# A layer's modulation in front of the recurrence's projections, and two block inverses with tiles of their own

## The chip, the cores and the metric

The kernel is one program on one core of a Trainium2 chip. What counts is the device time of one execution in microseconds (us). A core has engines that each run their own list of instructions in order: TensorE (PE, matrix products into the accumulator memory PSUM), VectorE (DVE), ScalarE (ACT), GpSimd (POOL) and SyncE (SP, which here only issues transfers from main memory, DMAs, into the on-chip memory SBUF). They meet at semaphores: an instruction waits until the data that it reads is there and the buffer that it writes is free.

## The reference

Two models run one after the other on a sequence `x` of 512 positions and 1024 channels. The change lies in the second, a two-layer model whose last layer is an RWKV-7 mixer. Cut to what matters:

```
mod = silu(c) @ mod_w[1] + mod_b[1]              # 6*1024 numbers: shift, scale, gate of the mixer, then of the FFN
u   = rmsnorm(x) * (1 + scale) + shift
xx  = 0.5 * (u shifted left + u shifted right) - u
k, v, r = (u + xx*mix[j]) @ w_rkv[j]             # 512x1024 by 1024x1024 each
decay_d = f(tanh(xw @ w1[d]) @ w2[d]); a_d = g((xa @ a1[d]) @ a2[d]); g = sigmoid(xg @ g1) @ g2
S_t = S_{t-1} * decay_t + (S_{t-1} @ -kk_t) (kk_t * a_t) + v_t k_t     # per head, forward and reversed
y_t = S_t @ r_t
x = x + gate * (readout(y) @ wo);   x = x + gate2 * swiglu(modulated x)
```

The gate of the mixer and the numbers of the FFN are only read after the recurrence.

## The kernel before

The recurrence is computed in blocks of 64 positions. Within a block the steps depend on each other through a triangular matrix for each head, which is inverted beforehand; the scan over the blocks is then matrix products. `rwkv_x` does this for `x`, after the same has been done for the context (the *context scan*, whose last instructions are L2583 on PE and L2587 on DVE). Its stages:

- `rwkv_branches` (L2071 and on): the norm of `x`, the mixes `u + xx*mix` (L2075, DVE), and linears of 1024 by 1024 in 8 column tiles, each weight tile loaded (`wraw<-rwkv_wrkv`, 512 KB) and split into a high and a low part (`whi` on ACT, `wlo` on DVE), then three products for every pair of tiles (L178 to L180). First comes the linear of k, with three narrow products beside it that the text calls loras: `lora_w`, `lora_a`, `lora_g`, each 24 matmuls into PSUM tag `aux`. The copy L2167 ends `lora_g`, the last of them. The linear of r and the rest follow.
- `rwkv_pairs` for direction 0, then `rwkv_values`; then `rwkv_inverse` for direction 0 (*inverse 0*), `rwkv_pairs` for direction 1 (which completes the matrix `AT1` with L2358), and `rwkv_inverse` for direction 1 (*inverse 1*). `self.pinv` (3 PSUM banks) is another pool for inverse 1 than for inverse 0.
- `rwkv_scan`, whose first products with the inverse are L2556 and L2558. Its products that need no inverse (L2526, L2540 on PE, L2531 and L2534 on DVE) may run earlier.

An inverse begins with transposes (L2382) and copies into `Am` (L2388 on ACT, L2390 on DVE), then a *chain* of 31 steps on DVE in which each step reads the one before (L2398 a product into `stmp`, L2400 a subtraction from `Tm`), and then a *tail*: transposes and small products on PE (L2410, L2430, L2447) whose results DVE and ACT copy out in turns (L2418, L2438, L2454 on DVE). A pool with one buffer for a tag makes a new tile of that tag wait for the last read of the one before: within an inverse, `TR` takes the tag of `Am`, and `US` that of `Tm`.

`modulation(1, nm1, 12, ...)` computes the last eight blocks (512 columns each) of the second layer's modulation, in two groups of four. For each of 32 loads:

```
raw = wraw()                                  # a buffer of tag wmod
nc.sync.dma_start(raw, w[:, g * 4:g * 4 + 4, c0:c0 + 256])           # L1418, 512 KB on SP's queue
for k in range(4):
    nc.tensor.matmul(ps[r:r + 32, ...], sc[:, c:c + 32], raw[:, k, :], ..., tile_position=(0, r))   # L1421
```

After 16 loads ACT copies the sum (`fmod`, L1427), PE multiplies it with a selection matrix (L1434), and DVE adds the bias (L1439). In the trace a load's four matmuls are eight records of L1421. The last group also gives `aff` (L1449, L1450). Nothing in `rwkv_x` reads the result before the readout.

The order of instructions on each engine is set by a scheduler that simulates the program; code that is written earlier is preferred where several instructions are ready. What came out is read from the compiled order below. `self.psums(sb, 3, 2)` gives three PSUM banks of tag `mm` and two of `aux` for the time of `rwkv_branches`.

Of the kernel before, what the change touches and what calls it, by code (L numbers as in the profile page):

```python
# [20 lines left out]
P = 128  # L21
# [82 lines left out]
class Kern:  # L104
# [2646 lines left out]
    def rwkv_x(self, x, rs, xs, xp, xd, sx):  # L2751
        nc = self.nc
        R = {}
        tile = lambda st, name, shape, side=None: self.t(self.pool(st, name, side=side), shape, tag=name)
        with ExitStack() as st:
            self.rp = self.pool(st, "rpx")
            self.rq = self.pool(st, "rqx")
            sv, sb = ExitStack(), ExitStack()
            self.weights_pool(sv, 2, 1024)
            self.work_pool(sv, 6)  # L2760
            self.nbc = 1
            ha = self.pool(sv, "heapv")
            v = self.fork(S)
            v.psums(sv, 2, 1, side="right")
            self.psums(sb, 3, 2)
            sh = ExitStack()
            self.rwkv_branches(x, S, 0, R, rs, (self.pool(sh, "heapb", side="right"), ha), xp)
            sh.close()
            sb.close()

            sr, sp_ = ExitStack(), ExitStack()
            A = [P, 32, 2, 64]
            AT = [tile(sr, "AT0", A, "right"), None]
            self.psums(sp_, 3, 2)
            sp = self.pool(sp_, "pairx", side="right")
            self.work_pool(sp_, 3, side="right")
            self.rwkv_pairs(R, S, 0, 0, AT[0], 0, sp)
            v.rwkv_values(R, S, 0)
            sv.close()
            si, s1 = ExitStack(), ExitStack()  # L2780
            self.pinv, self.pinv_tag = self.pool(si, self.nm("pinv"), 3, PSUM, "right"), "inv"
            DT = [tile(st, "DT0", [P, 64, 64]), None]
            AT[1] = tile(s1, "AT1", A)
            ip = self.pool(s1, "inv")
            self.rwkv_inverse(AT[0], DT[0], ip)
            self.rwkv_pairs(R, S, 0, 1, AT[1], 0, sp)
            sp_.close()
            sr.close()
            xs.close()
            DT[1] = tile(sr, "DT1", [P, 64, 64], "right")  # L2790
            sp = self.pool(sr, "scanx", side="right")
            sc = ExitStack()
            self.pmm = self.pool(sc, self.nm("scm"), 2, PSUM)
            si.close()
            self.paux = self.pool(sc, self.nm("sca"), 3, PSUM, "right")
            self.pinv = self.pool(s1, self.nm("pinv"), 3, PSUM)
            swm = ExitStack()
            wm = self.pool(swm, "wmod3", 1, side="right")
            self.rwkv_inverse(AT[1], DT[1], ip, 1)
            self.modulation(1, self.nm1, 12, (lambda: self.t(self.pmm, [P, 512], tag="aux"),  # L2800
                                              lambda: self.t(wm, [P, 4, 256], tag="wmod", bufs=4),
                                              lambda: self.t(wm, [P, 512], tag="fmod")))
            swm.close()
            s1.close()

            Y = [self.t(self.rq, [P, KC, 2, 2, 64], tag=f"rk{h}") for h in range(2)]
            self.weights_pool(st, 2)
            n = S // 64
            lag = self.lag
            steps = []  # L2810
            for i in range(n + lag):
                steps += [(0, i)] * (i < n) + [(1, i - lag)] * (i >= lag)
            with ExitStack() as s2:
                side = self.fork(S)
                side.work_pool(s2, 7)
                self.pyr = self.pool(s2, self.nm("scy"), 1, PSUM)
                side.paux = self.pmm
                self.rwkv_scan(R, S, 0, [(DT[0], 0), (DT[1], 0)], Y, sp, steps, side, self.pool(s2, "bon"))
            sr.close()
            sc.close()  # L2820
            self.psums(st, 4, 4)
            self.work_pool(st, 8)
            side = self.fork(S)
            side.work_pool(st, 6)
            self.heap(st, 18)
            xp = self.pool(sx, "xfin", side="right")
            x = []
            for k in range(KC):
                x.append(self.t(xp, [P, S], tag=f"x{k}"))
                nc.sync.dma_start(x[k], xd[k])  # L2830
            self.rsx = self.rwkv_readout(R, Y, x, side)
            return x
# [42 lines left out]
```

## Time and profile before

| | us |
|---|---|
| median of 3 runs (lowest, highest) | 3390.59 (3382.8, 3393.72) |
| profiled execution: its own time | 3386.3 |
| profiled execution: span | 3384.5 |
| PE busy | 3031.5 |
| DVE busy | 1901.3 |
| ACT busy | 1295.7 |
| mean granted TensorE clock, of full speed | 0.932 |

The span runs from the first to the last instruction of the profiled execution; its own time is 1.8 us longer. Busy times are sums over the whole span: an engine that is busy nine tenths of the time on average can still stand idle for tens of microseconds in one stage, so the stages around the change are read one by one. A row of windows (groups 1 and 10 below) gives for a stretch its limits and length, then the busy time (and the number of instructions) of PE, of its weight loads, of DVE, ACT and POOL, then TensorE's granted clock as a share of full speed, the busy share of the DMA engines, and GB/s.

### The profile page before, as it was taken

Reading aid. Unit: us, or ns where it says so; the run is one execution under the profiler, and the core shown is the slowest. Engines: PE = TensorE matmul, PEld = TensorE weight load, DVE = VectorE, ACT = ScalarE, POOL = GpSimd, SP = SyncE. Lnnn points to the kernel's source line nnn. Section 1 sums busy time; section 2 is a strip of 40 time slices with the busy share of each in tenths; the row PEclk is TensorE's granted clock in tenths of the full one; section 3 lists DMA queues with packets and bytes.
Section 4 is the critical chain, followed back from the end, with each engine's and each line's share of the span. In section 5 each row is a group of like instructions: output and inputs, shape, how many; then the busy total and the mean of one; then the engine's idle time right before and its main releaser. Section 6 shows DMA issues by size and latency. Waiting matters only on the chain.

```text
span 3384.5 us, 53425 instructions
## 1 busy us (share of the span) xinstructions
PE 3031.5 (90%) x21351; PEld 2320.5 (69%) x21351; DVE 1901.3 (56%) x3118; ACT 1295.7 (38%) x2378; POOL 568.9 (17%) x639
## 2 busy tenths in 40 slices
PE   8989799779999698999799999979977698889999
PEld 5667577544445677787588788866745587778887
DVE  5447553333333767666476776467795644753334
ACT  5335333213232445454344723335672132332222
POOL 2223210311111341000202300020361000310001
PEclk9989899889999799999899999989996589899999
DMA  6553564369997523334544532532775466442322
GB/s 215 172 184 113 191 210 158 112 230 359 360 304 244 170 79 107 110 102 121 171 130 126 146 92 75 136 91 81 207 200 174 112 167 156 129 131 90 97 92 71
DMA packets 537962, 526.04 MB, mean 155 GB/s; under 512 B 72289, under 2 KB 468795, under 8 KB 534640
## 3 DMA queue, kind: packets, MB, share of 16 engines
q1 hardware_dynamic: 512448, 449.77, 43.6%
q0 software_dynamic: 13840, 57.88, 5.1%
q10 hardware_dynamic: 11424, 14.96, 1.8%
q8 instruction: 169, 2.77, 0.4%
q14 instruction: 81, 0.66, 0.1%
HBM read 453.32 MB, written 69.21 MB: 154 GB/s over the span
## 4 chain that ended last, share of the span: by engine, by line
PE 43%; DVE 6%; DMA 5%; issue 3%; ACT 2%; POOL 1%; SPq 0%; ACTq 0%; DVEq 0%; POOLq 0%
PE mm L178 10%; PE mm L179 10%; PE mm L180 10%; PE inv L2447 1%; PE mm L1872 1%; DMA wmod<-mod_w 1%; PE aux L2526 1%; PE mm L2526 1%; DMA v<-vd 1%; PE big L1849 1%; PE aux L2572 1%; PE aux L2583 1%; PE yy L2558 1%; PE aux L1977 1%; DVE wlo L170 1%
## 5 line engine op out<-in xcount | busy, mean ns | idle before, releaser
L178 PE MATMUL mm<-s,whi 128*128 128x512 f32 (+1 forms) x2472 | 871.4, 357 | 48.1 <-ACT whi L169 15.8
L180 PE MATMUL mm<-s,wlo 128*128 128x512 f32 (+1 forms) x2472 | 872.1, 355 | 11.5 <-DVE wlo L170 11.1
L179 PE MATMUL mm<-s,whi 128*128 128x512 f32 (+1 forms) x2472 | 870.9, 353 | 11.4 <-DVE s L170 8.4
L169 ACT ACTIVATE whi<-wraw 128x1024 fp32r<-128x1024 f32 (+2 forms) x444 | 388.2, 882 | 862.1 <-PE mm L179 648.6
L170 DVE TENSOR_TENSOR wlo<-wraw,whi 128x1024 fp32r<-128x1024 f32 (+2 forms) x444 | 456.9, 1036 | 314.8 <-ACT whi L169 309.5
L178 PEld LDWEIGHTS mm<-s,whi 128*128 128x128 f32 x2472 | 473.8, 193 | 145.0 <-ACT whi L169 24.7
L180 PEld LDWEIGHTS mm<-s,wlo 128*128 128x128 f32 x2472 | 475.0, 192 | 90.1 <-DVE wlo L170 18.0
L179 PEld LDWEIGHTS mm<-s,whi 128*128 128x128 f32 x2472 | 475.8, 193 | 84.9 <-DVE s L170 13.2
L270 POOL TENSOR_TENSOR sq<-sq,w 128x512 f32<-128x512 f32 (+1 forms) x64 | 81.5, 1274 | 878.4 <-DVE w L266 787.7
L169 ACT ACTIVATE s<-w 128x512 fp32r<-128x512 f32 (+1 forms) x215 | 114.5, 546 | 90.2 <-POOL w L664 35.0
L170 DVE TENSOR_TENSOR s<-w,s 128x512 fp32r<-128x512 f32 (+1 forms) x215 | 128.4, 614 | 33.5 <-ACT s L169 32.9
L1659 DVE SCALAR_TENSOR_TENSOR x<-mm,mod,x 128x512 f32<-128x512 f32 (+1 forms) x128 | 89.8, 714 | 98.5 <-PE mm L180 97.9
L1330 PE MATMUL aux<-wgu,whi 128*64 128x512 f32 x496 | 131.9, 601 | 0.1
L1855 POOL TENSOR_SCALAR sst<-sst,hrs 128x1 f32<-128x1 f32 x96 | 33.7, 351 | 394.2 <-DVE sst L1853 345.6
L1346 PE MATMUL mm<-wraw,mt 128*64 128x512 f32 x248 | 89.7, 653 | 2.6 <-DVE mt L1340 2.6
L1700 DVE SCALAR_TENSOR_TENSOR w<-w,mm 128x512 f32<-128x512 f32 (+1 forms) x66 | 39.3, 596 | 91.0 <-PE mm L180 90.9
L1330 PEld LDWEIGHTS aux<-wgu,whi 128*64 128x64 f32 x496 | 39.7, 137 | 57.4 <-issue 52.4
L1977 PE MATMUL aux<-ident,pr 128*128 128x128 f32 x384 | 64.6, 277 | 6.5 <-ACT PT L1983 5.6
L1853 DVE TENSOR_REDUCE sst<-big 128x1 f32<-128x768 f32 x64 | 61.0, 953 | 12.9 <-PE big L1849 12.7
L2526 PE MATMUL aux<-LB,sbk 64*128 64x128 f32 x512 | 63.5, 307 | 3.5 <-DVE qq L2534 1.8
L1857 ACT ACTIVATE pr<-big,sst,hrs 128x768 f32<-128x768 f32 x64 | 63.1, 986 | 0.3 <-POOL sst L1855 0.3
L1849 PE MATMUL big<-kk,qs 128*128 128x512 f32 (+1 forms) x256 | 59.5, 356 | 3.9 <-ACT pr L1857 3.8
(711 smaller groups left out, 5365.7 us busy)
## 6 DMA issues: line engine op xcount, KB each, us to landing
wmod<-mod_w SPq DMA_DIRECT2D x80, 512.0 KB, 5.7
wraw<-w_down SPq DMA_DIRECT2D x31, 1024.0 KB, 10.7
wgu<-w_gate SPq DMA_DIRECT2D x56, 512.0 KB, 8.6
wgu<-w_up SPq DMA_DIRECT2D x56, 512.0 KB, 7.7
wraw<-ffn_wg SPq DMA_DIRECT2D x44, 512.0 KB, 3.9
wraw<-ffn_wu SPq DMA_DIRECT2D x44, 512.0 KB, 3.9
wraw<-ffn_wd SPq DMA_DIRECT2D x44, 512.0 KB, 3.8
wraw<-rwkv_wrkv SPq DMA_DIRECT2D x40, 512.0 KB, 4.0
```

The costliest lines, as they stand in the source:

```text
L169: nc.scalar.activation(hi, src, AF.Copy)
L170: nc.vector.tensor_tensor(lo, src, hi.bitcast(F32), op=ALU.subtract)
L178: nc.tensor.matmul(out, lh, rh, start=start, stop=False)
L179: nc.tensor.matmul(out, lh, rl, start=False, stop=False)
L180: nc.tensor.matmul(out, ll, rh, start=False, stop=stop)
L270: nc.gpsimd.tensor_tensor(acc, acc, q, op=ALU.add)
L1330: nc.tensor.matmul(pgu[i * 64:(i + 1) * 64, :], xs[:, k, i * 64:(i + 1) * 64], t[k // 4][:, k % 4, :], start=k == 0, stop=k == KC - 1)
L1346: nc.tensor.matmul(py[i * 64:(i + 1) * 64, :], mt[:, f, i * 64:(i + 1) * 64], d[:, f, q * 512:(q + 1) * 512], start=f == 0, stop=f == 1)
L1659: nc.vector.scalar_tensor_tensor(x[i], ps, self.mod[l][:, q * KC + i, c:c + 1], x[i], op0=ALU.mult, op1=ALU.add)
L1849: nc.tensor.matmul(ps[:, a:a + n], qs[i][:, e, c * P:(c + 1) * P], kk[g][q], start=q == 0, stop=q == 1)
L1977: nc.tensor.transpose(pp[:, k * P:(k + 1) * P], pr[:, (k0 + k) * P:(k0 + k + 1) * P], self.ident)
L2526: nc.tensor.matmul(pv[e][:, p, :NR].rearrange("p q t -> p (q t)"), bk[rows[e], 4 * h + p].rearrange("p s t -> p (s t)"), lb[e][rows[e], 4 ...
```

## The change

The eight blocks of modulation move from behind inverse 1 to the front of `rwkv_branches`. There they take their PSUM from tag `mm`, which the linears use, and have two buffers for their weights where they had four. The two inverses take `Am`, `Tm` and `stmp` from pools of their own (`inv0`, `inv1`), where one pool `inv` served both in turn.

```diff
--- before.py
+++ after.py
@@ -2763,9 +2763,14 @@
             v = self.fork(S)
             v.psums(sv, 2, 1, side="right")
             self.psums(sb, 3, 2)
-            sh = ExitStack()
+            sh, swm = ExitStack(), ExitStack()
+            wm = self.pool(swm, "wmod3")
+            self.modulation(1, self.nm1, 12, (lambda: self.t(self.pmm, [P, 512], tag="mm"),
+                                              lambda: self.t(wm, [P, 4, 256], tag="wmod", bufs=2),
+                                              lambda: self.t(wm, [P, 512], tag="fmod")))
             self.rwkv_branches(x, S, 0, R, rs, (self.pool(sh, "heapb", side="right"), ha), xp)
             sh.close()
+            swm.close()
             sb.close()
 
             sr, sp_ = ExitStack(), ExitStack()
@@ -2781,8 +2786,7 @@
             self.pinv, self.pinv_tag = self.pool(si, self.nm("pinv"), 3, PSUM, "right"), "inv"
             DT = [tile(st, "DT0", [P, 64, 64]), None]
             AT[1] = tile(s1, "AT1", A)
-            ip = self.pool(s1, "inv")
-            self.rwkv_inverse(AT[0], DT[0], ip)
+            self.rwkv_inverse(AT[0], DT[0], self.pool(s1, "inv0"))
             self.rwkv_pairs(R, S, 0, 1, AT[1], 0, sp)
             sp_.close()
             sr.close()
@@ -2794,13 +2798,7 @@
             si.close()
             self.paux = self.pool(sc, self.nm("sca"), 3, PSUM, "right")
             self.pinv = self.pool(s1, self.nm("pinv"), 3, PSUM)
-            swm = ExitStack()
-            wm = self.pool(swm, "wmod3", 1, side="right")
-            self.rwkv_inverse(AT[1], DT[1], ip, 1)
-            self.modulation(1, self.nm1, 12, (lambda: self.t(self.pmm, [P, 512], tag="aux"),
-                                              lambda: self.t(wm, [P, 4, 256], tag="wmod", bufs=4),
-                                              lambda: self.t(wm, [P, 512], tag="fmod")))
-            swm.close()
+            self.rwkv_inverse(AT[1], DT[1], self.pool(s1, "inv1"), 1)
             s1.close()
 
             Y = [self.t(self.rq, [P, KC, 2, 2, 64], tag=f"rk{h}") for h in range(2)]
```

How this stands in the compiled order, first on PE, at the end of the context scan. `aux_..<-v,tk` is the context scan's last product, `L241` the broadcast of the norm's factors, `mm<-s,whi` the linear of k. Before:

```order
L2583 MATMUL aux_17754<-v_3857_17674,tk_17700 64x64
L241 MATMUL aux_20331<-ident_63,rs_20280 128x128 x4
L178 MATMUL mm_20458<-s_20356,whi_20454 128x512
L178 MATMUL mm_20507<-s_20356,whi_20503 128x512
```

and of the changed kernel:

```order
L2583 MATMUL aux_17754<-v_3857_17674,tk_17700 64x64
L1421 MATMUL mm_20331<-wmod_20332,sc_1477 32x256 x4
L1421 MATMUL mm_20331<-wmod_20338,sc_1477 32x256 x4
L241 MATMUL aux_20549<-ident_63,rs_20280 128x128 x4
L1421 MATMUL mm_20331<-wmod_20344,sc_1477 32x256 x4
```

Two loads' matmuls of the modulation (`mm<-wmod,sc`) stand ahead of the broadcast, and more follow it. Further on, the last of the matmuls of `lora_a` (`aux<-s,lw`), the last nine loads of the modulation and the first matmuls of the linear of k, on PE in the changed kernel:

```order
L179 MATMUL aux_20892<-s_20991,lw_4466_20856 128x512
L180 MATMUL aux_20892<-s_20990,lw_4467_20857 128x512
L1421 MATMUL mm_20437<-wmod_20480,sc_1477 32x256 x4
L1421 MATMUL mm_20437<-wmod_20486,sc_1477 32x256 x4
L1421 MATMUL mm_20437<-wmod_20492,sc_1477 32x256 x4
L1421 MATMUL mm_20437<-wmod_20498,sc_1477 32x256 x4
...
L1421 MATMUL mm_20437<-wmod_20522,sc_1477 32x256 x4
L1421 MATMUL mm_20437<-wmod_20528,sc_1477 32x256 x4
L1434 MATMUL mm_20536<-qsel_70,fmod_20534 128x8 x4
L178 MATMUL mm_20676<-s_20574,whi_20672 128x512
L179 MATMUL mm_20676<-s_20575,whi_20672 128x512
```

All 32 loads' matmuls and the second L1434 now stand ahead of the linear's first one; `lora_w` and `lora_a` stand between load 12 and load 24, where they stood among the linear's matmuls. On SP, in the changed kernel, the loads with the fourth weight tile of the linear (`wraw<-rwkv_wrkv`) among them:

```order
L1418 DMA wmod_20462<-mod_w 128x4x256
L186 DMA wraw_20860<-rwkv_wrkv 128x8x128
L1418 DMA wmod_20468<-mod_w 128x4x256
L1418 DMA wmod_20474<-mod_w 128x4x256
...
L1418 DMA wmod_20522<-mod_w 128x4x256
L1418 DMA wmod_20528<-mod_w 128x4x256
L186 DMA wraw_20929<-rwkv_wrkv 128x8x128
```

Eleven loads of the modulation stand between the fourth and the fifth weight tile. SP takes its list in order, and a load that finds both buffers taken holds up what is behind it. On DVE, the end of chain 0 and what follows, before (`Am`, `Tm` and `stmp` of inverse 0):

```order
L2398 TENSOR_TENSOR stmp_22489<-Am_22340,Tm_22341 128x120
L2400 TENSOR_TENSOR Tm_22341<-Tm_22341,stmp_22489 128x2x2x30
L2398 TENSOR_TENSOR stmp_22492<-Am_22340,Tm_22341 128x62
L2400 TENSOR_TENSOR Tm_22341<-Tm_22341,stmp_22492 128x2x31
L2418 COPY Am_22495<-inv_22496 32x64x8
L2418 COPY Am_22495<-inv_22507 32x64x8
```

and of the changed kernel a little earlier in chain 0, where the copies into inverse 1's `Am` stand:

```order
L2390 COPY Am_23710<-inv_23765 64x2x128
L2400 TENSOR_TENSOR Tm_22560<-Tm_22560,stmp_22684 128x2x10x22
L2398 TENSOR_TENSOR stmp_23772<-Am_23710,Tm_23711 128x62
L2398 TENSOR_TENSOR stmp_22687<-Am_22559,Tm_22560 128x414
L2400 TENSOR_TENSOR Tm_23711<-Tm_23711,stmp_23772 128x2x31
L2400 TENSOR_TENSOR Tm_22560<-Tm_22560,stmp_22687 128x2x9x23
L2398 TENSOR_TENSOR stmp_23775<-Am_23710,Tm_23711 128x120
L2398 TENSOR_TENSOR stmp_22690<-Am_22559,Tm_22560 128x384
L2400 TENSOR_TENSOR Tm_23711<-Tm_23711,stmp_23775 128x2x30x2
```

The numbers behind the names tell the tiles apart: the steps of chain 1 (`Am_23710`, `Tm_23711`) now alternate with those of chain 0 from its step 9x23 on, where before they stood behind the whole tail of inverse 0.

## Rows read from the trace of the kernel before

**Rows 1.** Windows, beginning of the branches to the linears: busy us (instructions), clock, DMA

```profile
2263.00:2286.00 23.00, 14.89 (x43) 10.21 (x44) 23.00 (x30) 11.04 (x25) 6.27 (x5) 0.68 0.25 65
2350.00:2400.00 50.00, 49.97 (x207) 34.86 (x204) 21.26 (x27) 23.66 (x37) 10.53 (x1) 1.00 0.48 151
2400.00:2450.00 50.00, 47.34 (x275) 33.15 (x274) 40.17 (x40) 31.44 (x58) 20.82 (x14) 1.00 0.74 209
```

**Rows 2.** Timeline of PE: start us, us, instruction [idle before <-releaser]

```profile
2253.77 1.13 PE L241 MATMUL aux<-ident,rs 128*128 128x128 f32 x8 [0.88 <-DVE Sf L2587]
2263.43 0.79 PE L178 MATMUL mm<-s,whi 128*128 128x512 f32 x1 [8.53 <-ACT s L169]
...
2273.48 0.63 PE L178 MATMUL mm<-s,whi 128*128 128x512 f32 x1
2273.90 0.63 PE L179 MATMUL mm<-s,whi 128*128 128x512 f32 x1
...
2302.11 0.40 PE L178 MATMUL mm<-s,whi 128*128 128x512 f32 x1
2302.35 0.40 PE L179 MATMUL mm<-s,whi 128*128 128x512 f32 x1
```

**Rows 3.** Timeline of ACT: the copy that ends lora_g

```profile
2341.29 0.60 ACT L2167 ACTIVATE w<-aux 128x512 f32<-128x512 f32 x1 [3.36 <-PE aux L180]
```

**Rows 4.** The chain of waits, 2550 to 2730: start us, us, what

```profile
2557.90 3.68 DMA wmod<-mod_w
...
2655.68 0.61 ACT fmod L1427
2656.33 1.89 PE aux L1434 x8
```

**Rows 5.** Timeline of PE: the modulation's matmuls

```profile
2573.14 1.08 PE L1421 MATMUL aux<-wmod,sc 128*32 128x256 f32 x8 [0.41 <-DMA wmod<-mod_w]
2574.62 1.08 PE L1421 MATMUL aux<-wmod,sc 128*32 128x256 f32 x8 [0.40 <-DMA wmod<-mod_w]
```

**Rows 6.** Tile wmod, 2540 to 2660: transfer times

```profile
DMA to landing us min/median/max: 3.7/5.7/9.5
```

**Rows 7.** Timeline of ACT: the copy that completes AT1

```profile
2556.06 0.59 ACT L2358 ACTIVATE AT<-aux 64x512 f32<-64x512 f32 x1 [0.75 <-PE aux L2352]
```

**Rows 8.** Timeline of DVE: chain 0, chain 1, its tail

```profile
2567.62 0.62 DVE L2400 TENSOR_TENSOR Tm<-Tm,stmp 128x440 f32<-128x440 f32 x1
...
2576.31 0.22 DVE L2400 TENSOR_TENSOR Tm<-Tm,stmp 128x62 f32<-128x62 f32 x1
...
2630.00 1.11 DVE L2390 COPY Am<-inv 64x256 f32<-64x256 f32 x3 [2.44 <-ACT Am L2388]
...
2634.93 0.26 DVE L2398 TENSOR_TENSOR stmp<-Am,Tm 128x62 f32<-128x62 f32 x1
...
2658.25 0.26 DVE L1439 TENSOR_TENSOR mod<-aux,colt 128x16 f32<-128x16 f32 x2 [8.82 <-PE aux L1434]
...
2661.02 0.42 DVE L2534 TENSOR_TENSOR qq<-aux,mI 128x256 f32<-128x256 f32 x1
...
2684.13 0.22 DVE L2400 TENSOR_TENSOR Tm<-Tm,stmp 128x62 f32<-128x62 f32 x1
...
2707.06 0.70 DVE L2454 COPY DT<-inv 32x512 f32<-32x512 f32 x1 [2.34 <-PE inv L2447]
```

**Rows 9.** Timeline of PE: products in chain 1; first L2556

```profile
2665.06 1.09 PE L2540 MATMUL aux<-ident,sbk 128*128 128x128 f32 x4 [0.18 <-DVE qq L2534]
...
2667.33 3.09 PE L2526 MATMUL aux<-LB,sbk 64*128 64x128 f32 x16
...
2721.92 0.34 PE L2556 MATMUL yr<-v,LB 128*64 128x64 f32 x1 [0.88 <-DVE DT L2454]
```

**Rows 10.** Windows: second pairs, tail of inverse 0 (columns as in 1)

```profile
2500.00:2557.00 57.00, 31.38 (x275) 18.75 (x274) 56.43 (x63) 35.12 (x68) 31.67 (x21) 0.74 0.57 155
2577.00:2627.00 50.00, 45.24 (x906) 35.36 (x907) 15.86 (x27) 13.81 (x25) 2.44 (x4) 0.64 0.49 152
```


## The prediction

> **What bounds the kernel now.** I read the stages from the context scan's end to the scan of `x` in order: first the windows (which engine is full where), then the timelines of the engines that are waited for, then the chain of waits at the two places that the change touches.
>
> *The front.* PE leaves the context scan at 2253.77 and starts the linear of k at 2263.43 [rows 2]. In 2263 to 2286 DVE is full (23.00 of 23 us, mixes and splits) and PE is not (14.89) [rows 1]; from there on PE sets the pace. The copy that ends `lora_g`, the last of 264 matmuls (192 of the linear, 72 of three loras), starts at 2341.29 [rows 3]. PE is then full (49.97 of 50, 47.34 of 50) through the linears that follow [rows 1], so whatever comes later into 2341 is later by as much at 2450. The second pairs are DVE's: 56.43 of 57 us [rows 10].
>
> *The inverses.* `AT1` is complete at 2556.65 [rows 7], but the reader should see that inverse 1 cannot use it: chain 0 ends at 2576.5, and the copies into the shared `Am` stand at 2630, behind the tail of inverse 0 [rows 8]. In that tail PE is busy 45.24 of 50 us and DVE only 15.86 [rows 10]. Chain 1 runs from 2634.93 to 2684.35 with a stall of 8.82 us at a bias addition of the modulation, which waits for L1434 [rows 8]; the tail of inverse 1 then takes until the first L2556 at 2721.92 [rows 9], 37.6 us. The chain of waits goes through transfers of `wmod` [rows 4]. So two things lengthen this stretch, shared tiles and the modulation, and the change takes both away. It puts the modulation where PE waits 8.53 us and is then needed.
>
> **The loss at the front.** In the compiled order all 32 loads of the modulation are used on PE before the first matmul of the linear of k. The question is what a load costs there.
>
> A load alone took 3.68 us from issue to landing [rows 4], and its eight records 1.08 us [rows 5]. With four buffers the pitch was 2574.62 - 2573.14 = 1.48 us [rows 5]. With two buffers a load may be issued only when the matmuls of the load before the last are done, so a buffer goes round in 3.68 + 1.08 = 4.8 us at the least. Two transfers lie beside each other for a part of that, so I choose 5.1; two buffers then bring 2.55 us a load. Where nothing else is on PE this is its pace.
>
> - Loads 1 to 12: from 2254, 12 x 2.55 = 31 us, to 2285. DVE's mixes and the norm lie beside them, as they did beside the linear before.
> - Loads 13 to 23 with 48 matmuls of `lora_w` and `lora_a`: 11 x 1.08 = 12 us and, at the slow matmul pitch of 2273.90 - 2273.48 = 0.42 us [rows 2], 48 x 0.42 = 20 us; with the first L1434 and its copy (1.89 + 0.61 [rows 4]) and some 5 us for loads that are not there yet, 40 us, to 2325.
> - Loads 24 to 32 with nothing between: two have landed (2 x 1.08), seven come at 2.55: 20 us, then 2.5 for the copy and L1434. The linear of k starts at about 2347.
> - From there come 192 + 24 matmuls. At 2302.35 - 2302.11 = 0.24 [rows 2] they would be 52 us (the row is rounded; 50 us at 0.23), with some ten of them at 0.42 after PE's idle stretch 52 to 54. I take 52. Weight tiles, mixes and splits are early by then, so PE alone sets this. `lora_g` ends at 2399.
>
> 2399 against 2341.3: **58 us later**. PE's full stages carry this on; DVE, which ran ahead meanwhile, may give back up to the 2.7 us that PE stood idle in 2400 to 2450 [rows 1]. I take 55.
>
> Bounds: if the pitch were 1.48 also with two buffers, the three parts take 18 (but the first lora waits for the mixes of DVE, which is full until 2286 [rows 1]), 25 and 14 us, the linear starts at 2327, and the loss is 38. If a load took the median of 5.7 us [rows 6], which it took with four in flight, the pitch would be 3.45, the parts take 41, 46 and 29, and the loss is 81.
>
> Of the price of a load the Trainium skill ("DMA: Bandwidth & Descriptors", "Anatomy of one DMA") says that a transfer costs a fixed 2.0 us or so and the rest by size, and gives a fit; for 512 KB that would be an estimate of 3.2 us, and 2.2 us a load with two buffers. The row shows 3.68, and I keep the row. By the page the loss would be some 7 us less.
>
> **The gain at the inverses**, in the times of the trace before. Inverse 1 may start at 2556.65 [rows 7]. Its eight copies on DVE at 0.37 us (1.11 for three [rows 8]) stand in the order ahead of chain 0's step 9x23, which followed 2567.62 + 0.62 [rows 8]: it begins at about 2571. From there DVE has
>
> - the last nine steps of chain 0: 2576.53 - 2568.24 = 8.3 us [rows 8];
> - chain 1: 2684.35 - 2634.93 = 49.4, less the stall (8.8), the modulation's own additions (0.5) and 16 masks of the scan at 0.42 (6.7): 33.4 us [rows 8];
> - 20 copies of inverse 0's tail at 0.70: 14 us [rows 8].
>
> Together 56 us, so chain 1 ends at 2627 at the earliest; with some 11 us for copies that stand in line before their product is there (2.34 us before one of L2454 [rows 8]) at 2638. The tail of inverse 1 takes 37.6 us again and some 9 for scan products that now stand in it (five groups of L2526, 3.09 for two such, and four smaller L2540 [rows 9]), as chain 1 no longer leaves PE idle. First L2556 at about 2684.5 instead of 2721.9: **37 us earlier**. Bounds: 57 with no wait and no addition to the tail; 22 if the waits are twice as long and the tail 50 us.
>
> What hides the edit's small parts: the memsets of inverse 1's `Tm` on POOL (busy 2.44 of 50 us [rows 10]) now have no tile to wait for.
>
> **Sum.** 3386.3 (the profiled execution) + 55 - 37 = 3404. The median of the runs shown is 4.3 us above that execution, so 3408 stands for a median.
>
> **Rivals.**
>
> - *The loads come at the pace of bandwidth* (the other side). If two buffers suffice for 1.48 us a load, the loss is 38 and the gain 37: 3386.3 + 38 - 37 + 4.3 = 3392, no change, and 3372 with the gain at its upper bound. For it: the bandwidth is there, since DMA is busy only 0.25 of 2263 to 2286 [rows 1]. Against it: the first load's 3.68 us are mostly not bandwidth, as four in flight came every 1.48. A microsecond of pitch is worth (58 - 38) / 1.07 = 19 us here, so it decides below about 2.2 us a load, where 3408 falls under 3401. The Trainium skill's rule ("Trainium Kernel Development and Optimization", "Best Practices") to double-buffer so that transfers lie beside compute would say this; no row shows two buffers hiding transfers under matmuls of 1.08 us.
> - *The transfers are slower there*, since the linears' weights share SP's queue: 3.45 us a load, loss 81 less the same 3, gain 37: 3432. For it: weight loads stand among them in SP's order, as the fourth tile does in the rows of the change. Against: they have two buffers of their own, and at most two loads of the modulation are in flight where the 5.7 us were four.
> - *Inverse 1 does not get ahead*, because DVE is held by copies that wait for PE. Then only the stall (8.8) and the modulation's PE time in inverse 0's tail (45.2 against the 37.6 of the other tail) are saved: 16. 3386.3 + 55 - 16 + 4.3 = 3430. Against: in that tail DVE is free 34 of 50 us [rows 10], and the order interleaves the chains.
>
> **How the numbers follow.** This kernel's measurement tells about 0.3%, 10 us, from no change; so faster is below 3380, slower above 3401. The forecast with its own errors (3396 to 3420) has 0.45; the pace of bandwidth 0.33, of which 0.20 falls within 0.3% and 0.13 below it with a gain towards its bound; slower transfers 0.12; inverse 1 not ahead 0.10. Of the forecast's own 0.45, 0.03 lies between 3396 and 3401 and counts as no change: faster 0.13, same 0.20 + 0.03 = 0.23, slower 0.42 + 0.12 + 0.10 = 0.64. The range leaves out a tenth at each end: 3378 to 3432.
>
> **What would show it.** After the context scan, records of `mm<-wmod,sc` at a pitch of about 2.5 us (1.5: the first rival; 3.5: the second), each waiting for its transfer; the first `mm<-s,whi` some 90 us after L241, and L2167 52 us after that; PE full behind it. At the inverses, L2398 of the second `Am` before chain 0's end, its last step some 62 us after chain 0 would have ended alone, no L1439 there, and L2556 about 128 us after `AT1` (before 165). If L2167 comes less than 40 us later than before, or L2556 more than 150 us after `AT1`, a term of mine is wrong.

## The result and the profile after

The changed kernel takes 3406.18 us (median of 20 runs), the kernel before 3388.28 (20 runs beside them): ratio 1.0055, 95% interval 1.0042 to 1.0067. That is 18 us or 0.55% slower; 3408 was predicted for a median of 3390.6 before, 18 us more as well. The profiled execution has a span of 3406.3 us, 21.8 more than that of before.

The front first. PE's timeline of the changed kernel, with the matmuls of the first two loads, of the eighth from the end and of the last, and the first matmul of the linear of k (columns as in [rows 2]):

```profile
2259.79 1.07 PE L1421 MATMUL mm<-wmod,sc 128*32 128x256 f32 x16 [0.78 <-DVE Sf L2587]
...
2330.20 1.08 PE L1421 MATMUL mm<-wmod,sc 128*32 128x256 f32 x8 [1.35 <-DMA wmod<-mod_w]
...
2347.58 1.08 PE L1421 MATMUL mm<-wmod,sc 128*32 128x256 f32 x8 [1.66 <-DMA wmod<-mod_w]
...
2351.11 0.77 PE L178 MATMUL mm<-s,whi 128*128 128x512 f32 x1
```

Of the 32 loads 24 are waited for, and the last eight, with nothing between them, come at a pitch (the time from one load's matmuls to the next's) of (2347.58 - 2330.20) / 7 = 2.48 us. The whole modulation by tile, who waited for it (us, times) and the time from issue to landing of its transfers:

```profile
  PE mm L1421: 39.7, 24
...
DMA to landing us min/median/max: 3.4/4.3/6.7
```

The front is not of one piece. Windows of its beginning (loads 1 to 12) and of its end (columns as in [rows 1]):

```profile
2259.70:2294.00 34.30, 12.53 (x104) 3.35 (x104) 29.74 (x40) 16.38 (x36) 10.39 (x8) 0.58 0.86 240
2325.00:2351.00 26.00, 12.78 (x88) 4.55 (x87) 8.26 (x13) 7.05 (x12) 0.00 (x0) 0.60 0.58 182
```

At the beginning the linears' weights are loaded on the same queue and the DMA engines are busy for 0.86 of the time; the median time to landing is 4.8 us there and 3.7 at the end. Loads 3 to 12 come at (2292.84 - 2264.34) / 9 = 3.17 us. The first two had been issued at 2236.8, before the context scan ended, and cost no wait for a transfer.

ACT's timeline: the end of `lora_g`, the copy of the linear's last tile, and the completion of `AT1`:

```profile
2396.93 0.60 ACT L2167 ACTIVATE w<-aux 128x512 f32<-128x512 f32 x1 [1.48 <-PE aux L180]
...
2403.23 0.58 ACT L2141 ACTIVATE rk<-mm 128x512 f32<-128x512 f32 x1
...
2612.95 1.21 ACT L2358 ACTIVATE AT<-aux 64x512 f32<-64x512 f32 x2 [2.81 <-PE aux L2352]
```

In the changed order the last of the eight tiles stands behind `lora_g`, so L2141 here answers to [rows 3]: it starts at 2403.2, against 2341.3. Then the inverses. DVE's timeline has a copy into the second `Am` inside chain 0, a product of each chain in one row (the first of chain 1, and one of chain 0), and the last step of chain 1:

```profile
2621.36 0.43 DVE L2390 COPY Am<-inv 64x256 f32<-64x256 f32 x1
...
2629.53 0.75 DVE L2398 TENSOR_TENSOR stmp<-Am,Tm 128x62 f32<-128x62 f32 x2
...
2689.28 0.22 DVE L2400 TENSOR_TENSOR Tm<-Tm,stmp 128x62 f32<-128x62 f32 x1
```

and PE's the first L2556, 125.3 us after `AT1` (before 165.2, [rows 7, 9]):

```profile
2739.53 0.37 PE L2556 MATMUL yr<-v,LB 128*64 128x64 f32 x1 [2.02 <-DVE wlo L170]
```

Last the scan, which the prediction took as unchanged. Windows of the changed kernel and of the kernel before from the first L2556 to the scan's end (columns as in [rows 1]):

```profile
2739.50:2953.00 213.50, 185.11 (x3090) 164.30 (x3092) 107.91 (x213) 66.68 (x112) 25.78 (x35) 0.90 0.60 146
```

```profile
2722.00:2925.00 203.00, 177.37 (x3092) 156.87 (x3094) 109.30 (x214) 67.79 (x114) 25.76 (x35) 0.95 0.62 150
```

The same matmuls take PE 8 us longer at a mean granted clock of 0.90, and it is idle 3 us longer.

The span of each profiled execution, cut at five places that every kernel has: the context scan's end, the end of the linear of k with its three loras, `AT1`, the first and the last L2556. The stretches add up to the span; e1 to e12 are the experiments below, with their time as a ratio to the kernel before on the same chip.

| | context scan ends | front | to AT1 | inverses | scan | rest | ratio (95%) |
|---|---|---|---|---|---|---|---|
| before | 2253.6 | 87.7 | 215.4 | 165.2 | 200.1 | 462.5 | 1 |
| changed | 2259.7 | 143.5 | 211.0 | 125.3 | 210.5 | 456.3 | 1.0055 (1.0042-1.0067) |
| e1 | 2262.3 | 142.2 | 211.6 | 146.7 | 185.7 | 457.3 | 1.0073 (1.0057-1.0088) |
| e2 | 2266.6 | 87.4 | 216.3 | 126.6 | 205.0 | 456.7 | 0.9921 (0.9906-0.9936) |
| e3 | 2248.8 | 87.5 | 215.4 | 147.9 | 190.4 | 456.2 | 0.9933 (0.9913-0.9953) |
| e4 | 2255.1 | 151.0 | 214.9 | 123.9 | 205.7 | 456.7 | 1.0086 (1.0070-1.0102) |
| e5 | 2252.7 | 145.5 | 210.6 | 119.5 | 200.6 | 460.1 | 1.0013 (0.9998-1.0029) |
| e6 | 2253.0 | 87.7 | 214.0 | 166.2 | 193.3 | 456.6 | 0.9994 (0.9973-1.0015) |
| e7 | 2255.8 | 131.7 | 209.6 | 123.1 | 201.5 | 459.8 | 1.0005 (0.9988-1.0023) |
| e8 | 2251.1 | 87.7 | 215.9 | 160.6 | 201.8 | 459.1 | 1.0000 (0.9983-1.0017) |
| e9 | 2249.7 | 145.7 | 210.6 | 125.7 | 206.3 | 461.1 | 1.0064 (1.0038-1.0091) |
| e10 | 2250.5 | 141.7 | 211.9 | 147.0 | 219.9 | 458.2 | 1.0132 (1.0097-1.0166) |
| e11 | 2259.9 | 87.8 | 217.1 | 162.7 | 194.7 | 462.7 | 1.0007 (0.9986-1.0028) |
| e12 | 2257.5 | 145.4 | 210.6 | 127.0 | 197.4 | 458.2 | 1.0043 (1.0020-1.0066) |

Each row is one execution. The context scan ends between 2248.8 and 2266.6, though nothing ahead of it was changed (e5 and e6 alone change its loads of v, for which PE waits in none of these traces), and the rest varies by 6.5 us; so the 6.1 us by which the changed kernel's context scan ended later, and the 6.2 by which its rest was shorter, are no effect that one profile can show. The front is steadier (87.4 to 87.8 in the six kernels without the modulation there, 141.7 to 145.7 in the six with it and two buffers). The scan is not: kernels that do its products on PE in nearly the same order, with as many buffers, differ by 5 to 9 us (210.5, 205.0 and 201.5 in the changed kernel, e2 and e7; 200.1 and 205.7 in the kernel before and e4; 185.7 and 190.4 in e1 and e3). One profile therefore hardly tells 10 us in the scan from chance, but it does tell 25.

### The profile page after: what moved, and what is told of

It reads as the page before. It is cut to its first block, busy times and chain, and to the rows that moved or that the text cites. A ratio compares the mean times of both kernels' runs of the same rounds, so it can differ in the third digit from the quotient of the medians.

```text
span 3406.3 us, 53433 instructions
## 1 busy us (share of the span) xinstructions
PE 3042.5 (89%) x21351; PEld 2326.1 (68%) x21351; DVE 1896.6 (56%) x3118; ACT 1297.4 (38%) x2378; POOL 572.4 (17%) x639
## 4 chain that ended last, share of the span: by engine, by line
PE 44%; DVE 6%; DMA 5%; issue 2%; ACT 1%; POOL 0%; SPq 0%; ACTq 0%; DVEq 0%; POOLq 0%
PE mm L178 10%; PE mm L179 10%; PE mm L180 10%; PE aux L2526 1%; DMA wmod<-mod_w 1%; PE mm L1872 1%; DMA v<-vd 1%; PE inv L2447 1%; DVE stmp L2398 1%; PE mm L2526 1%; DVE Tm L2400 1%; PE big L1849 1%; PE aux L2572 1%; PE aux L2583 1%; PE aux L1977 1%
## 5 line engine op out<-in xcount | busy, mean ns | idle before, releaser
L180 PEld LDWEIGHTS mm<-s,wlo 128*128 128x128 f32 x2472 | 472.1, 191 | 83.8 <-DVE wlo L170 11.5
L1330 PEld LDWEIGHTS aux<-wgu,whi 128*64 128x64 f32 x496 | 39.7, 137 | 57.4 <-issue 52.6
L2526 PE MATMUL aux<-LB,sbk 64*128 64x128 f32 x512 | 67.2, 320 | 9.5 <-DMA v<-vd 4.4
L1853 DVE TENSOR_REDUCE sst<-big 128x1 f32<-128x768 f32 x64 | 60.9, 952 | 12.8 <-PE big L1849 12.6
L2526 PEld LDWEIGHTS aux<-LB,sbk 64*128 64x128 f32 x512 | 58.0, 219 | 13.9 <-issue 6.3
L1421 PE MATMUL mm<-wmod,sc 128*32 128x256 f32 x256 | 29.9, 560 | 40.6 <-DMA wmod<-mod_w 39.7
```

The costliest lines, as they stand in the source:

```text
L180: nc.tensor.matmul(out, ll, rh, start=False, stop=stop)
L1330: nc.tensor.matmul(pgu[i * 64:(i + 1) * 64, :], xs[:, k, i * 64:(i + 1) * 64], t[k // 4][:, k % 4, :], start=k == 0, stop=k == KC - 1)
L1853: nc.vector.tensor_reduce(st[:, 0:1], ps, AX.X, ALU.max)
L2526: nc.tensor.matmul(pv[e][:, p, :NR].rearrange("p q t -> p (q t)"), bk[rows[e], 4 * h + p].rearrange("p s t -> p (s t)"), lb[e][rows[e], 4 ...
```

## The experiments

**e1: only the modulation moved, one pool for both inverses.** On the changed kernel:

```diff
-            self.rwkv_inverse(AT[0], DT[0], self.pool(s1, "inv0"))
+            ip = self.pool(s1, "inv")
+            self.rwkv_inverse(AT[0], DT[0], ip)
...
-            self.rwkv_inverse(AT[1], DT[1], self.pool(s1, "inv1"), 1)
+            self.rwkv_inverse(AT[1], DT[1], ip, 1)
```

> The modulation stands in front as in the changed kernel, but the two inverses share one pool of tiles as before. Theory (own tiles bring about 22 of the 40 us by which the stretch from AT1 to the first L2556 is shorter, the modulation's leaving the rest): about 22 us slower than the changed kernel, 1.2% slower than the kernel before; chain 1 starts behind the tail of inverse 0, and the stretch takes about 148 us. Rival (the shorter stretch is all due to the modulation having left it, the tiles do nothing): as the changed kernel, 0.55% slower than before, stretch 125 us.

Measured: the stretch at the inverses is 146.7 us, as the theory had it, but the kernel is not 22 us slower than the changed one; the intervals overlap. The scan took 185.7 us, 25 less than in the changed kernel, and PE's row of waits for v there is a quarter of what it was:

```profile
PE yy L2558 <- DMA v<-vd: 3.4, 3, 1.9
```

against the changed kernel's

```profile
PE yy L2558 <- DMA v<-vd: 14.8, 7, 4.3
```

and the 12.9 us of the kernel before. So own tiles bring the first L2556 forward by 21 us, and the scan behind it gives that back. PE's window of e1's scan, to set beside the two above, shows 10 us less of busy time and 15 us less of idle time than the changed kernel's:

```profile
2762.80:2951.50 188.70, 175.43 (x3090) 156.41 (x3092) 109.27 (x214) 67.32 (x114) 25.78 (x35) 0.96 0.67 161
```

**e2 and e3: no modulation, with own tiles and with shared ones.** The call of `modulation` is replaced, in the changed kernel and in the kernel before, by copies of the bias (the eight blocks' loads and products are left out):

```diff
-            self.modulation(1, self.nm1, 12, ...)
+            md, bias = self.mod[1], self.cols["mod_b1"]
+            for s in range(2):
+                nc.vector.tensor_copy(md[:, 4 * self.nm1:48, s], bias[:, 4 * self.nm1:48])
```

(and the two small operations that make `aff` of it).

> The changed kernel without the eight blocks' loads and products: their place in the modulation holds the bias alone. Theory (the modulation costs its whole 50 us or so in front, nothing hides it): about 52 us faster than the changed kernel, 3354, 1.0% faster than the kernel before; the linear of k starts about 10 us after the context scan. Rival (most of those 50 us would pass anyway, because mixes and weight tiles are not there earlier): less than 25 us faster than the changed kernel.

> The kernel before without the eight blocks' loads and products, the bias alone in their place; the inverses share their tiles. Theory (in its old place the modulation costs the stall of 8.8 us in chain 1 and some 8 in the tail of inverse 0): 16 us faster than the kernel before, 0.5%. Rival (the modulation was what kept inverse 1 late): 35 to 40 us faster, 1.1%.

Measured: 0.9921 and 0.9933. In front the modulation costs 1.0055 - 0.9921 = 1.3%, some 45 us (36 to 55 by the ends of the intervals); in its old place 0.7%, some 23 us (16 to 29). The first expectation's theory holds, with 45 where it said 52; of the second, 16 is at the edge and the rival's 35 to 40 outside. In e3 the inverses' stretch is 17.3 us shorter than before, which is what the prediction gave the modulation's leaving (16), and the scan is 9.7 us shorter besides. Own tiles against shared ones without any modulation: 21.3 us less at the inverses, 14.6 more in the scan, and times that cannot be told apart: the second pair that shows it.

**e4 and e7: three buffers in front.** e4 frees the room by putting the copy `fmod` into a work tile, e7 by putting it into a load buffer for a moment (e7's edit, cut):

```diff
-                                              lambda: self.t(wm, [P, 4, 256], tag="wmod", bufs=2),
-                                              lambda: self.t(wm, [P, 512], tag="fmod")))
+            raw = lambda: self.t(wm, [P, 4, 256], tag="wmod", bufs=3)
...
+                                              lambda: raw().rearrange("p k c -> p (k c)")[:, :512]))
```

> The changed kernel with three buffers for the modulation's weights (the copy fmod goes to a work tile to make room). Theory (the pace in front is a load's time from issue to release, divided by the number of buffers): the pitch falls from 2.5 to 1.7 us a load, the 32 loads take about 55 us with nothing between them, the linear of k starts 12 to 20 us earlier, and the kernel is by about 15 us faster than the changed one, level with the kernel before. Rival (the pace is set by the transfers' bandwidth beside the linears' weights, or by PE): pitch and time as in the changed kernel.

Measured: a miss, 1.0086. The pitch fell to (2322.86 - 2305.37) / 9 = 1.94 us and the linear began 16 us earlier, but the front took 151.0 us. PE's timeline, and the window of the modulation in e4, which shows DVE idle:

```profile
2305.37 1.08 PE L1421 MATMUL mm<-wmod,sc 128*32 128x256 f32 x8 [1.32 <-DMA wmod<-mod_w]
...
2322.86 1.08 PE L1421 MATMUL mm<-wmod,sc 128*32 128x256 f32 x8 [0.72 <-DMA wmod<-mod_w]
```

```profile
2255.00:2325.00 70.00, 35.42 (x274) 9.78 (x274) 6.90 (x11) 4.75 (x6) 0.00 (x0) 0.56 0.87 255
```

6.90 of 70 us, where the changed kernel's DVE did mixes (29.74 in its first 34.3 us). DVE waited 52.1 us, in two waits, for the modulation's L1434, to make its additions L1439. The work tile that `fmod` took is one of those that the mixes go through in turn; they stood behind it, the loras behind them, and both then fell into the linear. The edit had a second effect, so it says little on the first.

> As the run with three buffers, but the copy fmod takes a load buffer for a moment and no work tile, so that DVE's mixes are not held back and the two loras stand among the loads again. Theory (pitch of loads): 1.9 us a load, the linear of k starts about 77 us after the context scan (91 with two buffers) and ends about 130 after it (143.5), and the kernel is 12 us faster than the changed one if the scan's order stays. Rival (the front is bound by PE or DVE work beside the loads): the linear of k ends within 5 us of the changed kernel's 143.5.

Measured: as the theory has it. PE's timeline of e7, last two loads and first matmul of the linear:

```profile
2329.47 0.64 PE L1421 MATMUL mm<-wmod,sc 128*32 128x256 f32 x8 [1.86 <-DMA wmod<-mod_w]
2331.59 0.64 PE L1421 MATMUL mm<-wmod,sc 128*32 128x256 f32 x8 [1.49 <-DMA wmod<-mod_w]
...
2334.68 0.77 PE L178 MATMUL mm<-s,whi 128*128 128x512 f32 x1
```

The linear starts 78.8 us after the context scan (91.4 with two buffers) and the front takes 131.7 us (143.5). PE's waits for loads fell from 39.7 to 25.4 us. With 1.0005 the kernel is level with the one before. Of the 17 us between it and the changed kernel the front has 12; its scan was 9 us shorter in the profile as well, with nearly the same order, and that is no effect of the buffer that one profile shows. So one more buffer of 4 KB a partition gives back 12 us in front; that it is worth the whole loss of the change is not shown.

**e5 and e6: v loaded by SP**, in the changed kernel and in the kernel before:

```diff
-                nc.scalar.dma_start(v2[o].rearrange("t q p k -> t q (p k)"),
+                nc.sync.dma_start(v2[o].rearrange("t q p k -> t q (p k)"),
```

> The changed kernel, but the scan's loads of v are issued by SP, where ACT issued them between its own copies. Theory (the 21 us that own tiles bring until the first L2556 are lost again inside the scan, because the order that the scheduler gives ACT there issues v late: PE's wait for v is 14.8 us and the clock falls behind it): that wait falls below 5 us, the scan from the first to the last L2556 takes about 190 us instead of 210, and the kernel is 15 to 20 us faster than the changed one, level with the kernel before. Rival (the scan is longer because masks and products that ran beside chain 1 alone are now left for it): the wait for v goes, but the scan takes 205 us or more and the time is within 6 us of the changed kernel's.

> The kernel before, with the scan's loads of v issued by SP. Theory (the kernel before has the same order on ACT in most steps and waits 12.9 us for v): the wait falls below 5 us, the scan takes about 188 us instead of 200, and the kernel is about 11 us faster than before. Rival: within 5 us of before.

Measured: e5 is faster than the changed kernel (1.0013 against 1.0055), and its scan 10 us shorter, but not for the reason given: PE still waits 12.9 us for v (e6: 10.1, and no gain in time that can be measured). What SP itself waited for in e5's scan tells why:

```profile
SPq L2516 <- PE yy L2593: 69.0, 14, 8.0
```

The loads of v (L2516) wait for the last product of an earlier step, which frees their buffer. Not the queue is late but the buffer. My theory on ACT's list fell here. What made e5 faster stays open: PE is idle no less in its scan than in the changed kernel's (30.0 and 28.4 us), its busy time is 11 us shorter at a clock of 0.94 where the changed kernel had 0.90, and its inverses took 6 us less.

**e12: a third buffer for one of the two tiles of v:**

```diff
-                v2 = self.t(sp, [P, 2, KC, 64], tag=f"v{e}", bufs=2)
+                v2 = self.t(sp, [P, 2, KC, 64], tag=f"v{e}", bufs=3 - e if read else 2)
```

> The changed kernel with three instead of two buffers for one of the two tiles of v in the scan (there is room for one); the compiled order of PE stays as it is. Theory (with ends back to back a load of v waits for the release of its buffer at the end of the step before the last, and lands too late): about half of the waits for v go, 14.8 to 8 us, and the scan is 5 to 10 us shorter. Rival (the loads are late because of their place in ACT's list or because of the transfers beside them): wait and scan as in the changed kernel.

Measured, with the same order of the scan's products on PE as in the changed kernel (but for a few neighbours that changed places):

```profile
PE yy L2558 <- DMA v<-vd: 6.5, 5, 1.9
```

The wait is halved and the scan 13 us shorter in the profile (197.4). In time it is 1.0043 against 1.0055, with overlapping intervals: that it makes the kernel faster is not shown.

**e9 and e10: the scan's order.** In the compiled order of e1 and e3 PE alternates between the two directions for most of the scan (between a step's L2572 and its L2583 stand L2526 and L2558 of other steps); before and after the change it mostly does L2583 and L2593 of both directions back to back (at 12 places in either), and then waits for the loads of v behind both. The edit is one number, how many steps the second direction is written behind the first:

```diff
-        self.lag = 3
+        self.lag = 2
```

> The changed kernel with one number of the scan changed: the second direction's steps are written 2 instead of 3 steps behind the first's. In the compiled order PE then alternates between the two directions (products of one between the products of the other) in more of the steps, and in 8 instead of 12 places it does the ends of two steps back to back with the next loads of v behind both. Theory (the scan's time hangs on that order, back-to-back ends leave PE waiting for v): the wait for v falls from 14.8 to about 10 us, the scan from the first to the last L2556 from 210 to about 200, and the kernel is some 8 us faster than the changed one. Rival (the scan is longer because work that used to lie beside chain 1 is left for it): scan and time within 4 us of the changed kernel's.

> The kernel with the modulation in front and shared tiles, whose scan alternated in nearly all steps and took 185.7 us, with the lag of 2, which here gives fewer alternating steps (8 places with ends back to back instead of 6). Theory (order): the scan takes 192 us or more, the wait for v rises from 3.4 us, and the kernel is some 8 us slower than with the lag of 3. Rival (shared tiles leave the scan better prepared, whatever its order): the scan stays within 4 us of 185.7.

Measured: e9 is a miss for the theory, the wait fell to 12.6 and the scan to 206.3 us, the time is the changed kernel's. e10 speaks clearly for it: the same kernel as e1 but for the lag, the inverses take the same 147.0 us, and the scan 219.9 us instead of 185.7:

```profile
PE yy L2558 <- DMA v<-vd: 16.7, 7, 4.4
```

It is 0.6% slower than e1, with intervals that do not touch. That it is the order that came with the lag, and not the lag by itself, is argued from e9, where the same lag cost nothing. But I expected it of 8 places back to back instead of 6, and e9 with as many had 206.3 us: counting such places does not give the size.

**e8 and e11: the modulation beside the second pairs**, with own tiles and four buffers, e11 with the lag of 2 as well (the call in front goes; this is what comes in its place):

```diff
             self.rwkv_pairs(R, S, 0, 1, AT[1], 0, sp)
+            wm = self.pool(sp_, "wmod3", side="right")
+            self.modulation(1, self.nm1, 12, (lambda: self.t(self.pmm, [P, 512], tag="mm"),
+                                              lambda: self.t(wm, [P, 4, 256], tag="wmod", bufs=4),
+                                              lambda: self.t(wm, [P, 512], tag="fmod")))
```

> Own tiles for the inverses, and the modulation written behind the second pairs, with four buffers and PSUM tag mm: its loads stand among the second pairs, chain 0 and the tail of inverse 0, where PE is busy 31 of 57 us. Theory (the modulation costs what stands in the way of an engine that is waited for, and here PE has room): it costs at most 15 us against the changed kernel without modulation (0.992 of before), so 1.0 to 0.5% faster than the kernel before. Rival (its loads and matmuls delay the tail of inverse 0 and the transfers of the pairs as much as in front): no faster than the kernel before.

> Own tiles, the modulation written behind the second pairs with four buffers, and the lag of 2, which here gives the alternating order in most steps (6 places with ends back to back). Theory (order): the scan takes about 188 us instead of 202 with the lag of 3, and the kernel is 0.4% faster than the kernel before, so faster than both. Rival: the scan takes 198 us or more, level with the kernel before.

Measured: 1.0000 and 1.0007, level with the kernel before; both theories missed. In e8 own tiles were of no use: the copies into the second `Am` stand behind the tail of inverse 0 again, as DVE's timeline shows (chain 0 had ended at 2575.0):

```profile
2627.07 0.43 DVE L2390 COPY Am<-inv 64x256 f32<-64x256 f32 x1 [0.63 <-ACT Am L2388]
```

In e11 the scan was 7 us shorter than in e8, without a gain in time. No kernel here with its whole computation beats the one before.

## Why the prediction was right, and where not

**The front: 58 predicted, 55.8 measured** (143.5 - 87.7). Of its three parts, loads 1 to 12 took 34 us (predicted 31), loads 13 to 23 with the loras 33 (40), and the rest until the linear 24 (22), 91.4 together where 93 was said. That the sum fits better than its parts is luck. In the first part the pitch was 3.17 and not 2.55, and the two loads that had come before the context scan's end, which I did not count, made up for most of it. In the second, 20 of the 48 matmuls of the loras came 0.23 us apart, at full clock, and not 0.42. The third was too short because I counted two of its loads as landed; the first of them was still waited for (1.34 us). There the pitch shows by itself, 2.48 for 2.55.

That two buffers' pitch is a buffer's round trip and not bandwidth is shown by that stretch, with DMA busy for 0.58 of it and every load waited for, and by e4, where a third buffer brought 1.94; in the trace of before four buffers came at 1.48 [rows 5]. The load of [rows 4] was not alone, as three more were issued within 1.6 us behind it; its 3.68 us are still near the median of 3.7 with two in flight. The Trainium skill ("DMA: Bandwidth & Descriptors", "Anatomy of one DMA") led to an estimate of 2.2 us for two buffers; its fit is one for transfers issued from GpSimd, these are issued by SP, the trace shows 2.48, and the measurement decides. The marker of the prediction was named wrongly: L2167 came 46 us after the linear's start, since a tile of the linear stands behind it; the linear itself took the 52.

**Carried on: 55 predicted, 51.4 measured** at `AT1` (211.0 - 215.4 = 4.4 given back where I took 3).

**The inverses: 37 predicted, 39.9 measured.** The parts hold too: with shared tiles 18.5 us are left (e1), so own tiles make 21.4 of it; the third rival's 16 for the modulation's leaving alone is near e3's 17.3. Chain 1 ended 75.3 us after `AT1` (2689.5 - 2614.2), where I said 81.4 (2638 - 2556.6); from there the first L2556 took 50.0, where I said 46.6.

**The step that was missing: the scan.** The sum took what is gained at the first L2556 as gained at the end. The scan then took 25 us more than with shared tiles (e1), and two pairs of kernels (changed and e1, e2 and e3) show that the tiles' 21 us at the inverses bring no time that can be measured. The scan is no block of fixed length: it took from 185.7 to 219.9 us. e10 points to the order, e12 in the profile to the buffers of v. What share of the 25 us is PE's wait (14.8 - 3.4 = 11.4) and what the clock behind it is not settled: PE's busy time for the same products was 185.1 us at a clock of 0.90 in the changed kernel, and 175.4 at 0.96 in e1. Against the kernel before, the changed kernel's scan is 10.4 us longer; its order has the same 12 places back to back, the wait for v is only 2 us longer, and what made the rest, if it is more than chance, stays open.

**The sum.** In the profiles 6.1 + 55.8 - 4.4 - 39.9 + 10.4 - 6.2 = 21.8; the first and the last term vary so much between executions of other kernels that I give them to no cause. In medians it is 18. By my three terms alone it would have been 11.5. The runs without the modulation split the 18 another way: in front it costs 45 us, its old place gave back 23, and own tiles bring some 4 (e2 against e3, -8 to 16 by the ends of the intervals). I had lost 55 and gained 37, of which the third rival's 16 for the modulation's leaving makes the tiles' part 21. The difference came out right, and part of that is luck: the loss may be what I said (36 to 55), the modulation's leaving brought 16 or more, and the tiles, whose 21 us the profile shows at the inverses, brought little or nothing of it at the end.

**The rivals.** The pace of bandwidth was false with two buffers. The price of a microsecond of pitch (19 us) is not borne out: in e7 the 32 loads came 0.39 us closer on average and the front is 12 us shorter, which makes 31. It hung on the lower bound, whose 25 us for the second part and 2327 for the linear do not follow from the terms given. Slower transfers were right for loads 3 to 12, with a pitch of 3.17 near the 3.45 of that rival, and false behind them. Inverse 1 did get ahead.

## What to carry to other kernels

A modulation that "only" streams weights costs the round trip of its buffers wherever an engine's list puts its matmuls ahead of what is needed next: divide a load's time from issue to release by the number of buffers before moving it, and look what else is loaded beside it; here one more buffer took 12 us of 56 off the front. And follow a gain to the end of the stage behind it: a scheduler that orders the whole program may pay for an earlier start with a worse order, as with own tiles against shared ones here, so compare that stage's order and waits, and not only when it begins. A sum that comes out right can have wrong terms: time the kernel without each part as well.

## What the runs showed of the hardware

In the scan the granted clock was mostly lower where PE waited longer for v, and the same products mostly took it longer: a wait of 3.4 us with a mean clock of 0.96 and 175.4 us busy (e1), 14.8 with 0.90 and 185.1 (changed kernel), 16.7 with 0.86 and 197.8 (e10). The wait alone does not set it: the kernel before waited 12.9 us with 0.95 and 177.4. In the front the eight records of a load took 1.08 us where the granted clock was 0.50 (1.2 GHz; 2330.2 to 2347.6 of the changed kernel, PE busy 7.6 of 17.4 us), and 0.64 where it was 1.00 (2.4 GHz; 2326.9 to 2332.2 of e7, behind matmuls of the loras without a gap).

A third buffer brought the pitch from 2.48 to 1.94 us and not to two thirds of it (1.65), since the transfers took longer: the median time to landing was 3.7 us in the last stretch of the changed kernel and 4.7 in that of e4. With the 1.08 us of the matmuls, (3.7 + 1.08) / 2 = 2.4 and (4.7 + 1.08) / 3 = 1.9.
